# Hymba block on one core: the weight quarters of a Strassen unit are prepared in step with its products

## The chip, the cores and the metric

The kernel runs on one core of one Trainium2 chip. The metric is device time in microseconds (us); the time of a kernel is the median of its runs. A profile is one execution taken by the hardware profiler.

## What is computed

One decoder block over 2048 positions, 1024 features wide, in float32. Cut to what matters here:

```python
h = rmsnorm(x, norm1_g)
proj = h @ w_in                       # 1024 -> 3088 columns: q, k, v, g, a, c_b, c_c, c_h
o = rmsnorm(gla_chunked(q, k, v, log_a)) * silu(g)      # gated linear attention, chunked
o_conv = c_b * causal_depthwise_conv(c_c * c_h)         # the short convolution
x = x + concat(o, o_conv) @ w_out
h2 = rmsnorm(x, norm2_g)
x = x + (silu(h2 @ w_ffn_gate) * (h2 @ w_ffn_up)) @ w_ffn_down   # 1024 -> 2816 -> 1024
out = rmsnorm(x, norm_f_g)
```

## The kernel before

**Halves and units.** The sequence is worked in two halves of 1024 positions. Every large matrix product is cut into units. A unit is a 2 by 2 block product by a Strassen-Winograd scheme with seven products instead of eight (`PRODUCTS`): A11·B11, S1·T1, S2·T2, A12·B21, S3·T3, S4·B22, A22·T4. The A side is weights: four raw quarters A11, A12, A22, A21, and the sums S1 to S4, which VectorE (DVE) makes in place from the raw quarters (four operations, line 435). The B side is activations, the operands (`op`), in the same eight forms.

**Split floats.** Each float32 value is used as a high and a low part. `split` makes them: the high part by ScalarE (ACT, line 193), the low part by DVE as the difference (line 194). `product_step` issues three matmuls for each step of 128 in the contracted dimension: high by high, high by low, low by high (lines 460 to 462). A product is 12 matmuls in the input projection and in the FFN's up-projection (four steps), and 6 or 9 in the down-projection (two or three steps, with quarters 256 or 384 columns wide).

**A unit's life.** `raw_weights` loads the four raw quarters with one DMA (pool `rawp`, two buffers; 1024 KB, or 512 and 768 KB in the down-projection). `weight_quarter` splits a quarter into a tile of pool `wqp`, which has four buffers: the split of one quarter can begin when the product four before it has read its own. `unit_weights` writes the whole sequence of splits and sums of a unit ahead of its products: A11, the sums for S1, S2 and S3, S1, S2, A12, S3, the sum for S4, S4, A22. Then `unit` makes the products into PSUM banks and takes the results out: products 0, 1 and 2 by a copy on ACT (`copied`, line 500), later ones by a sum on DVE (`plus`, line 489). Products 0, 2, 4 and 6 accumulate into one bank, 1 and 5 into another, so product 2 must wait for the copy of product 0, product 4 for that of product 2, and so on. In the down-projection the results are mostly added onto a running sum y by DVE (`onto`).

**The order of the kernel.** Opening (norm, transposes, the first input-projection units 0 to 2), the other input-projection units of half 0 (3 to 11) and of half 1 (0 to 11) with the gated attention and its gates worked in between, the output projection, then for each half the FFN: `ffn_up`, 22 units (11 pairs of gate and up), and `ffn_down`, four groups of contracted steps (`GROUPS` = 0, 2, 5, 8) with four units each. The last unit of all, `last_unit`, uses plain quarters without Strassen. The operands of the down-projection were stored to DRAM by `ffn_up`; those named T3, B22 and T4 come back unsplit and are split after the load by ACT and DVE. `load_h2` loads the operands of half 1's up-projection.

**What sets the order on each engine.** A list scheduler with a model of times goes through the program and orders the instructions of each engine by their place in the program and by when they can run. `tc.issue_after` and the helper `behind` only fix which of two instructions of one engine is issued first; they add no semaphore. Each engine works its queue in order, so an instruction that waits holds everything queued behind it on its engine.

Of the kernel before, what the change touches and what calls it, by code (L numbers as in the profile page):

```python
# [11 lines left out]
F32 = mybir.dt.float32  # L12
# [8 lines left out]
P = 128  # L21
D = 1024
SEQ = 2048
PB = 512
# [29 lines left out]
def tile_hymba_block(ctx, tc, x, xt, win, wa, wgu, wout, wffn, wdown, wdown_first, small, out):  # L54
# [270 lines left out]
    def no_operands():  # L325
        return {b: [] for _, b in PRODUCTS}
# [91 lines left out]
    def unit_weights(src, raw=None, between=()):  # L418
# [33 lines left out]
        halves.clear()  # L452
        return w

    def product_step(o, w, op, k, first):
        n = len(op)
        c = slice(k * P, (k + 1) * P)
        wh, wl = w[:, 0, c], w[:, 1, c]
        xh, xl = op[k][:, 0, :], op[k][:, 1, :]
        pe.matmul(o[:], wh, xh, start=first and k == 0, stop=False, skip_group_check=True)  # L460
        pe.matmul(o[:], wh, xl, start=False, stop=False, skip_group_check=True)  # L461
        return pe.matmul(o[:], wl, xh, start=False, stop=k == n - 1, skip_group_check=True)  # L462

    def unit(src, ops, into=None, onto=None, raw=None, between=(), rest=None):

        w = unit_weights(src, raw, between)
        unit_splits[:] = last_hi + last_lo
        with behind(unit_splits):  # L470
            for y, o in unsplit:
                split(y[:], o[:, 0, :], o[:, 1, :])
        unsplit.clear()

        def mul(i, o=None):
            first = o is None
            o = bank() if first else o
            n, m = PRODUCTS[i]
            for k in range(len(ops[m])):
                product_step(o, w[n], ops[m], k, first)  # L480
            tick()
            return o

        def plus(t, o):
            if ordered:
                queued(dve, lambda: dve.tensor_tensor(t[:], o[:], t[:], ALU.add))
            else:
                with behind(held if rest is not None else []):
                    last_plus[:] = [dve.tensor_tensor(t[:], o[:], t[:], ALU.add)]  # L489
            return t  # L490

        def then():
            if rest is not None:
                next(rest)

        def copied(name, o, at):
            if onto is not None:
                return plus(onto[at], o)
            t = tt(name) if into is None else into[at]
            last_out[:] = [act.activation(t[:], o[:], AF.Copy)]  # L500
            return t


        oa = mul(0)
        c11 = copied("c11", oa, (0, 0))
        ob = mul(1)
        c22 = copied("c22", ob, (1, 1))
        mul(2, oa)
        c12 = copied("c12", oa, (0, 1))
        o = mul(3)  # L510
        then()
        plus(c11, o)
        mul(4, oa)
        then()
        plus(c22, oa)
        if rest is not None:
            next(rest, None)
            w["A22"] = weight_quarter(w["A22"])
            held[:] = last_hi + last_lo
            ordered.clear()  # L520
        mul(5, ob)
        plus(c12, ob)
        mul(6, oa)
        if into is not None or onto is not None:
            copied("c21", oa, (1, 0))
        return [(0, 0, c11, False), (1, 1, c22, False), (0, 1, c12, False), (1, 0, oa, True)]

    def settled(c, in_psum):
# [480 lines left out]
    def in_proj(half, ops, raw=None, between=(), rest=None):  # L1009
        def units():  # L1010
            if half == 0:
                yield unit(win[2], ops, raw=raw, between=between, rest=rest)
            for u in range(0 if half else 3, 12):
                yield unit(win[u], ops)

        units = units()
        for dst, i0 in ((s_kq, 0), (s_kq, 2), (s_v, 0), (s_v, 2)):
            if half == 0 and dst is s_kq:
                continue
            for r, j, c, p in next(units):  # L1020
                store(dst[2 * half + j][i0 + r][:], settled(c, p)[:])
        for i0 in (0, 2):
            for r, j, c, p in next(units):
                store(s_g[2 * half + j][i0 + r][:], silu(c, p)[:])
        if half:
            background.append(gla_half(half))
        for i0 in (0, 2):
            cc = {(r, j): settled(c, p) for r, j, c, p in next(units)}
            ch = {(r, j): c for r, j, c, _ in next(units)}
            for r in range(2):  # L1030
                i = i0 + r
                left = halo[:, i, :]
                for j in range(2):
                    s = tp.tile([P, PB + 2], F32, name="u", tag="t")
                    dve.tensor_tensor(s[:, 2:], ch[r, j][:], cc[r, j][:], ALU.mult)
                    act.activation(s[:, 0:2], left, AF.Copy)
                    left = s[:, PB : PB + 2]
                    y = cc[r, j]
                    act.activation(y[:], s[:, 0:PB], AF.Copy, scale=col(C_CW + i))
                    for n in (1, 2):  # L1040
                        dve.scalar_tensor_tensor(
                            y[:], s[:, n : n + PB], col(C_CW + 4 * n + i), y[:], ALU.mult, ALU.add
                        )
                if half == 0:
                    act.activation(halo[:, i, :], left, AF.Copy)
            for r, j, c, _ in next(units):
                y = cc[r, j]
                dve.tensor_tensor(y[:], c[:], y[:], ALU.mult)
                hi = tp.tile([P, PB], F32R, name="hi", tag="t")
                split(y[:], hi[:], y[:].bitcast(F32R))  # L1050
                dst = s_mix[2 * half + j][i0 + r]
                store(dst[:, 0, :], hi[:].bitcast(F32))
                store(dst[:, 1, :], y[:])
# [239 lines left out]
        yield from combine(lambda k, j: s_x1[2 + j][k][:], C_G2, rb, put)  # L1293

    def load_h2():
        ops, loads = no_operands(), raw_loads[-2]
        for _, n in PRODUCTS:
            for k in range(4):
                with tc.issue_after(loads.ins):
                    o = (load_whole if n in WHOLE else load_pair)(s_h2p[n][k])  # L1300
                ops[n].append(o)
        return ops

    def ffn_up(half, ops):
        for m in range(NF // 2):
            us = unit(wffn[2 * m], ops)
            sg = {(r, j): silu(c, p) for r, j, c, p in us}
            for r, j, c, _ in unit(wffn[2 * m + 1], ops):
                s = sg[r, j]
                dve.tensor_tensor(s[:], c[:], s[:], ALU.mult)  # L1310
            b11, b12, b21, b22 = [sg[r, j] for r in range(2) for j in range(2)]
# [24 lines left out]
    def act_op(half, m, n):  # L1336
        return (load_whole if n in WHOLE else load_pair)(s_act[half][m][n])

    def ffn_down(half):
# [6 lines left out]
        for u, m0 in enumerate(GROUPS):  # L1346
            ms = range(m0, m0 + (3 if u else 2))
            last = m0 == LAST_GROUP
            if last:
                drain_background()  # L1350
            raw = None
            if u:
                raw = raw_weights(wdown[4 * u - 4])
                with tc.issue_after(raw_loads[-1].ins):
                    ops = {n: [group_op(m, n) for m in ms] for _, n in PRODUCTS}
            else:
                ops = {n: [group_op(m, n) for m in ms] for _, n in PRODUCTS}
# [3 lines left out]
                    tiny.tile([P, PB], F32, name=f"ssx{j}", tag=f"ssx{j}", bufs=1) for j in range(2)  # L1361
                ]
            for d0 in range(0, KD, 2):
                src = wdown[4 * u - 4 + d0 // 2] if u else wdown_first[d0 // 2]
                if u == 0 and d0 == 2:

                    order = [(m, n) for _, n in PRODUCTS for m in range(GROUPS[1], GROUPS[2])]
# [2 lines left out]
                if u == 0:  # L1370
                    for d in (d0, d0 + 1):
                        if d < KD - 1:
                            pair = opp.tile([P, 2, PB], F32, name="y", tag="op")
                        for j in range(2):
                            y[d, j] = pair[:, j, :] if d < KD - 1 else bt("y")[:]
                    unit(src, ops, {(r, j): y[d0 + r, j] for r in range(2) for j in range(2)})
                    continue
                xs = []
                if u < 3:
# [1 line left out]
                        xs.append((y[d, u - 1], bt("x1")))  # L1381
                        load(xs[-1][1][:], s_x1[2 * half + u - 1][d][:])
                if last and half and d0 == KD - 2:
                    last_unit(src, ops, [act_op(half, m, "B12") for m in ms], y, ssq)
                    break
                onto = {(r, j): y[d0 + r, j] for r in range(2) for j in range(2)}
                unit(src, ops, onto=onto, raw=None if d0 else raw)
                for r, j in ((0, 0), (1, 1), (0, 1), (1, 0)):
                    yy = onto[r, j]
                    if last and half:  # L1390
# [24 lines left out]
                dve.scalar_tensor_tensor(y[:], y[:], col(C_GF + d), rb[:], ALU.mult, ALU.mult)  # L1415
                store(out[2 * half + j, :, d, :], y[:])

    def last_unit(src, ops, b12, y, ssq):


        raw = raw_weights(src)
        w = [weight_quarter(raw[:, i, :]) for i in (0, 1, 3, 2)]
        columns = (ops["B11"], ops["B21"]), (b12, ops["B22"])
        def gain(d, j):
            return act.activation(y[d, j], y[d, j], AF.Copy, scale=col(C_GF + d))
# [101 lines left out]
        ctx.enter_context(tc.tile_pool(name=n, bufs=bufs, reuse_waits="tile"))  # L1527
        for n, bufs in (("fx", 11), ("fo", 3))
    ]
    for half in range(2):  # L1530
        ffn_up(half, load_h2() if half else h2)
        ffn_down(half)
# [106 lines left out]
```

## Time and profile before

| | before |
|---|---|
| median of 3 runs | 2059.78 us (2059.01 to 2061.59) |
| the profiled execution | 2056.94 us, its span 2055.2 us |
| granted TensorE clock | 0.995 |
| ScalarE table loads at line 540 | 8, of 1283 ns each |
| operations in the splits at line 193 (raw quarters) | 612, 587 ns each |
| their low parts at line 194 | 612, 739 ns each |

In a profile PE is TensorE's matmuls, PEld its weight loads, DVE VectorE, ACT ScalarE, POOL GpSimd and SP the queue that issues the DMAs. A row of the timeline gives the start (us from the start of the span), the duration, the engine, the source line, the operation and its tiles, output left of the arrow; in brackets how long the engine was idle before it and what ended that. Equal neighbours are put together (x2). A row of the waits gives an engine's line, what it waited for, the total, the number of waits and the longest. Lines are those of the kernel before.

### The profile page before, as it was taken

Reading aid. Unit: us, or ns where it says so; the run is one execution under the profiler, and the core shown is the slowest. Engines: PE = TensorE matmul, PEld = TensorE weight load, DVE = VectorE, ACT = ScalarE, POOL = GpSimd, SP = SyncE. Lnnn points to the kernel's source line nnn. Section 1 sums busy time; section 2 is a strip of 40 time slices with the busy share of each in tenths; the row PEclk is TensorE's granted clock in tenths of the full one; section 3 lists DMA queues with packets and bytes.
Section 4 is the critical chain, followed back from the end, with each engine's and each line's share of the span. In section 5 each row is a group of like instructions: output and inputs, shape, how many; then the busy total and the mean of one; then the engine's idle time right before and its main releaser. Section 6 shows DMA issues by size and latency. Waiting matters only on the chain.

```text
span 2055.2 us, 27032 instructions
## 1 busy us (share of the span) xinstructions
PE 2024.1 (98%) x9271; PEld 1664.6 (81%) x9271; DVE 1548.4 (75%) x2533; ACT 979.9 (48%) x1934; POOL 336.4 (16%) x218
## 2 busy tenths in 40 slices
PE   9999999999999999999999999999999999999997
PEld 8778878787888888888888888887888878888886
DVE  7878976569743787887786788877777777778884
ACT  6665455766543344444444552335544544453344
POOL 0000000000002451232131112201312221211213
PEclk9999999999999999999999999999999999999999
DMA  7356786425686873555454676576544534486663
GB/s 261 116 196 214 281 303 194 140 75 170 221 275 218 327 273 123 207 182 205 159 181 147 236 277 253 190 279 249 180 148 169 188 125 169 168 323 215 241 226 117
DMA packets 189738, 422.54 MB, mean 206 GB/s; under 512 B 19904, under 2 KB 65184, under 8 KB 180128
## 3 DMA queue, kind: packets, MB, share of 16 engines
q1 hardware_dynamic: 189600, 420.81, 57.8%
q8 instruction: 73, 1.20, 0.2%
q14 instruction: 65, 0.53, 0.1%
HBM read 276.02 MB, written 144.70 MB: 205 GB/s over the span
## 4 chain that ended last, share of the span: by engine, by line
PE 86%; DVE 5%; DMA 4%; ACT 3%; issue 2%; SPq 0%; POOL 0%; DVEq 0%; ACTq 0%; POOLq 0%
PE mm L460 25%; PE mm L462 24%; PE mm L461 24%; DMA op<-sa_T 2%; PE mm L1201 2%; PE mm L1202 2%; PE mm L1204 2%; DVE wq L194 1%; DMA raw<-in_wffn_dram 1%; DVE h L882 1%; PE a_ps L958 1%; PE mm L744 1%; PE mm L746 1%; PE mm L745 1%; PE o_ps L1125 1%
## 5 line engine op out<-in xcount | busy, mean ns | idle before, releaser
L460 PE MATMUL mm<-op,wq 128*128 128x512 f32 x2467 | 961.7, 393 | 13.7 <-ACT c L500 6.6
L461 PE MATMUL mm<-op,wq 128*128 128x512 f32 x2467 | 960.8, 390 | 0.2 <-DVE op L194 0.2
L462 PE MATMUL mm<-op,wq 128*128 128x512 f32 x2467 | 951.2, 390 | 0.5 <-DVE wq L194 0.2
L193 ACT ACTIVATE wq<-raw 128x512 fp32r<-128x512 f32 (+2 forms) x612 | 355.4, 587 | 588.3 <-PE mm L462 456.5
L194 DVE TENSOR_TENSOR wq<-raw,wq 128x512 fp32r<-128x512 f32 (+2 forms) x612 | 449.1, 739 | 179.7 <-ACT wq L193 177.8
L460 PEld LDWEIGHTS mm<-op,wq 128*128 128x128 f32 x2467 | 464.2, 188 | 118.2 <-ACT c L500 8.5
L462 PEld LDWEIGHTS mm<-op,wq 128*128 128x128 f32 x2467 | 464.2, 188 | 100.1 <-DVE wq L194 2.4
L461 PEld LDWEIGHTS mm<-op,wq 128*128 128x128 f32 x2467 | 464.3, 188 | 96.1 <-DVE op L194 1.3
L1183 POOL TENSOR_TENSOR ssx<-ssx,q 128x512 f32<-128x512 f32 x52 | 74.8, 1453 | 867.6 <-ACT q L1182 867.4
L489 DVE TENSOR_TENSOR c<-mm,c 128x512 f32<-128x512 f32 x196 | 134.8, 688 | 56.2 <-PE mm L462 53.7
L489 DVE TENSOR_TENSOR y<-mm,y 128x512 f32<-128x512 f32 x185 | 126.5, 687 | 47.4 <-PE mm L462 47.1
L435 DVE TENSOR_TENSOR raw<-raw 128x512 f32<-128x512 f32 (+2 forms) x192 | 151.7, 794 | 3.2
L1314 POOL TENSOR_TENSOR t<-c,c 128x512 f32<-128x512 f32 x44 | 73.9, 1678 | 432.0 <-DVE c L1310 409.7
L500 ACT ACTIVATE c<-mm 128x512 f32<-128x512 f32 x198 | 115.5, 588 | 19.0 <-PE mm L462 15.8
L1201 PE MATMUL mm<-op,wq 128*128 128x512 f32 x256 | 100.7, 395 | 0.0
L435 DVE TENSOR_TENSOR s<-raw 128x512 f32<-128x512 f32 (+2 forms) x96 | 64.1, 668 | 48.3 <-DMA raw<-in_wffn_dram 23.7
L1202 PE MATMUL mm<-op,wq 128*128 128x512 f32 x256 | 99.9, 390 | 0.0
L193 ACT ACTIVATE wq<-s 128x512 fp32r<-128x512 f32 (+2 forms) x96 | 56.2, 586 | 88.9 <-PE mm L462 85.3
L1396 POOL TENSOR_TENSOR y<-x,y 128x512 f32<-128x512 f32 x32 | 58.3, 1823 | 229.8 <-DVE y L489 163.7
L1204 PE MATMUL mm<-op,wq 128*128 128x512 f32 x256 | 79.9, 390 | 0.0
L435 DVE TENSOR_TENSOR raw<-s,raw 128x512 f32<-128x512 f32 (+2 forms) x96 | 69.8, 727 | 1.9
L194 DVE TENSOR_TENSOR op<-op 128x512 fp32r<-128x512 f32 x94 | 62.0, 686 | 5.3 <-ACT op L193 5.0
(230 smaller groups left out, 1777.4 us busy)
## 6 DMA issues: line engine op xcount, KB each, us to landing
raw<-in_wffn_dram SPq DMA_DIRECT2D x44, 1024.0 KB, 6.1
sa_B<-so SPq DMA_DIRECT2D x47, 512.0 KB, 3.4
op<-sa_B SPq DMA_DIRECT2D x47, 512.0 KB, 7.1
raw<-in_win_dram SPq DMA_DIRECT2D x22, 1024.0 KB, 5.4
sa_T<-so SPq DMA_DIRECT2D x44, 512.0 KB, 4.2
op<-sa_T SPq DMA_DIRECT2D x44, 512.0 KB, 6.6
raw<-in_wdown_dram SPq DMA_DIRECT2D x24, 768.0 KB, 5.6
sx<-y SPq DMA_DIRECT2D x48, 256.0 KB, 4.2
```

The source lines that it names most:

```text
L193: last_hi[:] = [act.activation(hi, src, AF.Copy)]
L194: last_lo[:] = [dve.tensor_tensor(lo, src, hi.bitcast(F32), ALU.subtract)]
L435: dve.tensor_tensor(*args)
L460: pe.matmul(o[:], wh, xh, start=first and k == 0, stop=False, skip_group_check=True)
L461: pe.matmul(o[:], wh, xl, start=False, stop=False, skip_group_check=True)
L462: return pe.matmul(o[:], wl, xh, start=False, stop=k == n - 1, skip_group_check=True)
L489: last_plus[:] = [dve.tensor_tensor(t[:], o[:], t[:], ALU.add)]
L500: last_out[:] = [act.activation(t[:], o[:], AF.Copy)]
L1183: pool.tensor_tensor(ssq[:], ssq[:], q[:], ALU.add)
L1201: pe.matmul(o[e, j][:], wh, m[:, 0, :], start=k == 0, stop=False)
L1202: pe.matmul(o[e, j][:], wh, m[:, 1, :], start=False, stop=False)
L1204: pe.matmul(o[e, j][:], wl, ops[k][j][:, 0, :], start=False, stop=k == KD - 1)
```

## The change

The weights of all units after the opening's are no longer prepared by the unit itself. A generator, `weight_flow`, goes over a list of weight sources, once for the input projection and once for the whole FFN, both halves, and yields once per quarter. `begin_flow` starts it with four credits; `advance` runs it as far as credits allow; after each product's copy or sum `unit` calls `freed`, which gives one credit (for the narrow quarters of group 0, of which two share a tile, one for every two). So the split of quarter p + 4 is written right behind the copy or sum of product p, and fixed behind it on its engine by `behind(last_out + last_plus)`. The sums stand with the splits: the sum that makes S1 behind the split of A11, the two others ahead of the split of S1, the last with S3. The raw load of the next unit is written when a unit's flow begins, so that the flow is two loads ahead (`Begun`). `load_h2` is put behind an earlier weight load (`raw_loads[-4]`), the operand loads of the down-projection behind the load of the unit that is just beginning, and `last_unit` finds its quarters already made.

```diff
+    plan, begun_units, credits, flowing = deque(), deque(), [0], []
+    class Begun:
+        def __init__(self, src):
+            self.raw = raw_weights(src)
+            self.load = raw_loads[-1]
+            self.w, self.narrow = {}, src.shape[-1] == PB // 2
+    def weight_flow():
+        following = Begun(plan.popleft())
+        while following is not None:
+            u, following = following, None
+            begun_units.append(u)
+            if plan:
+                following = Begun(plan.popleft())
...
+                s1 = rawp.tile([P, PB], F32, name="s1", tag="s1", bufs=1)[:, 0:n]
+                jobs = [
+                    ("A11", a11, [(s1, a21, a22, ALU.add)]),
+                    ("S1", s1, [(a21, a11, a21, ALU.subtract), (a11, s1, a11, ALU.subtract)]),
+                    ("S2", a11, ()), ("A12", a12, ()),
+                    ("S3", a21, [(a12, a12, a11, ALU.subtract)]), ("S4", a12, ()),
+                    ("A22", a22, ()),
+                ]
+            for i, (name, part, sums) in enumerate(jobs):
+                yield not (u.narrow and i % 2)
+                with behind(last_out + last_plus):
+                    if name == "S1":
+                        for job in sums:
+                            dve.tensor_tensor(*job)
+                    w[name] = weight_quarter(part)
+                    if name != "S1":
+                        for job in sums:
+                            dve.tensor_tensor(*job)
...
+    def advance():
+        while flowing:
+            fresh = flowing[1]
+            if fresh and not credits[0]:
+                return
+            credits[0] -= fresh
+            flowing[1:] = [next(flowing[0], None)]
+            if flowing[1] is None:
+                flowing.clear()
+    def begin_flow(sources):
+        plan.extend(sources)
+        credits[0] = 4
+        flow = weight_flow()
+        flowing[:] = [flow, next(flow)]
+        advance()
...
-        w = unit_weights(src, raw, between)
+        flows = src is None
+        if flows:
+            current = begun_units.popleft()
+            w = current.w
+        else:
+            w = unit_weights(src, raw, between)
...
+        def freed(i):
+            if flows and flowing:
+                if not current.narrow or i % 2 or i == len(PRODUCTS) - 1:
+                    credits[0] += 1
+                advance()
...
         oa = mul(0)
         c11 = copied("c11", oa, (0, 0))
+        freed(0)
         ob = mul(1)
         c22 = copied("c22", ob, (1, 1))
+        freed(1)
...
-        ops, loads = no_operands(), raw_loads[-2]
+        ops, loads = no_operands(), raw_loads[-4]
...
-                raw = raw_weights(wdown[4 * u - 4])
-                with tc.issue_after(raw_loads[-1].ins):
+                with tc.issue_after(begun_units[0].load.ins):
                     ops = {n: [group_op(m, n) for m in ms] for _, n in PRODUCTS}
...
-    def last_unit(src, ops, b12, y, ssq):
-        raw = raw_weights(src)
-        w = [weight_quarter(raw[:, i, :]) for i in (0, 1, 3, 2)]
+    def last_unit(ops, b12, y, ssq):
+        w = [begun_units[0].w[i] for i in (0, 1, 3, 2)]
```

More of the change, by code (lines that the diff above doesn't have):

```diff
@@ L453, in unit_weights @@
         return w
+    plan, begun_units, credits, flowing = deque(), deque(), [0], []
[11 more added lines that the diff above has]
+                following = Begun(plan.popleft())
+            raw, w, n = u.raw, u.w, u.raw.shape[-1]
+            a11, a12, a22, a21 = [raw[:, i, :] for i in range(4)]
+            if following is None and last_plain:
+                jobs = [(i, raw[:, i, :], ()) for i in (0, 1, 3, 2)]
+            else:
[17 more added lines that the diff above has]
+                            dve.tensor_tensor(*job)
+            halves.clear()
+    last_plain = []
+    def advance():
[13 more added lines that the diff above has]
+        advance()
     def product_step(o, w, op, k, first):
@@ L464, in unit @@
     def unit(src, ops, into=None, onto=None, raw=None, between=(), rest=None):
-        w = unit_weights(src, raw, between)
+        flows = src is None
+        if flows:
+            current = begun_units.popleft()
+            w = current.w
+        else:
+            w = unit_weights(src, raw, between)
         unit_splits[:] = last_hi + last_lo
@@ L505, in unit @@
         c11 = copied("c11", oa, (0, 0))
+        freed(0)
         ob = mul(1)
         c22 = copied("c22", ob, (1, 1))
+        freed(1)
         mul(2, oa)
         c12 = copied("c12", oa, (0, 1))
+        freed(2)
         o = mul(3)
@@ L512, in unit @@
         plus(c11, o)
+        freed(3)
         mul(4, oa)
@@ L515, in unit @@
         plus(c22, oa)
+        freed(4)
         if rest is not None:
@@ L522, in unit @@
         plus(c12, ob)
+        freed(5)
         mul(6, oa)
@@ L525, in unit @@
             copied("c21", oa, (1, 0))
+        freed(6)
         return [(0, 0, c11, False), (1, 1, c22, False), (0, 1, c12, False), (1, 0, oa, True)]
@@ L1012, in units @@
                 yield unit(win[2], ops, raw=raw, between=between, rest=rest)
+                begin_flow([win[u] for h in range(2) for u in range(0 if h else 3, 12)])
             for u in range(0 if half else 3, 12):
-                yield unit(win[u], ops)
+                yield unit(None, ops)
         units = units()
@@ L1305, in ffn_up @@
         for m in range(NF // 2):
-            us = unit(wffn[2 * m], ops)
+            us = unit(None, ops)
             sg = {(r, j): silu(c, p) for r, j, c, p in us}
-            for r, j, c, _ in unit(wffn[2 * m + 1], ops):
+            for r, j, c, _ in unit(None, ops):
                 s = sg[r, j]
@@ L1350, in ffn_down @@
                 drain_background()
-            raw = None
             if u:
-                raw = raw_weights(wdown[4 * u - 4])
-                with tc.issue_after(raw_loads[-1].ins):
+                with tc.issue_after(begun_units[0].load.ins):
                     ops = {n: [group_op(m, n) for m in ms] for _, n in PRODUCTS}
@@ L1363, in ffn_down @@
             for d0 in range(0, KD, 2):
-                src = wdown[4 * u - 4 + d0 // 2] if u else wdown_first[d0 // 2]
                 if u == 0 and d0 == 2:
@@ L1375, in ffn_down @@
                             y[d, j] = pair[:, j, :] if d < KD - 1 else bt("y")[:]
-                    unit(src, ops, {(r, j): y[d0 + r, j] for r in range(2) for j in range(2)})
+                    unit(None, ops, {(r, j): y[d0 + r, j] for r in range(2) for j in range(2)})
                     continue
@@ L1383, in ffn_down @@
                 if last and half and d0 == KD - 2:
-                    last_unit(src, ops, [act_op(half, m, "B12") for m in ms], y, ssq)
+                    last_unit(ops, [act_op(half, m, "B12") for m in ms], y, ssq)
                     break
                 onto = {(r, j): y[d0 + r, j] for r in range(2) for j in range(2)}
-                unit(src, ops, onto=onto, raw=None if d0 else raw)
+                unit(None, ops, onto=onto)
                 for r, j in ((0, 0), (1, 1), (0, 1), (1, 0)):
@@ L1529, in tile_hymba_block @@
     ]
+    last_plain.append(True)
+    begin_flow(
+        [
+            w
+            for _ in range(2)
+            for w in (
+                *[wffn[u] for u in range(NF)],
+                *[wdown_first[d] for d in range(4)], *[wdown[d] for d in range(12)],
+            )
+        ]
+    )
     for half in range(2):
```

## The prediction

> **What bounds the kernel now.** I read the page's first part, then its chain, then what TensorE (PE) waited for.
>
> ```profile
> span 2055.2 us, 27032 instructions
> PE 2024.1 (98%) x9271; PEld 1664.6 (81%) x9271; DVE 1548.4 (75%) x2533; ACT 979.9 (48%) x1934; POOL 336.4 (16%) x218
> ...
> PE 86%; DVE 5%; DMA 4%; ACT 3%; issue 2%; SPq 0%; POOL 0%; DVEq 0%; ACTq 0%; POOLq 0%
> ```
>
> PE is busy for 98% of the span and carries 86% of the chain. The change leaves every matmul in place, so all that it can win lies in the 2055.2 - 2024.1 = 31.1 us in which PE is idle, plus stretches in which PE runs slowly after a wait. What it can lose has no such ceiling. The windows of time show where PE is idle at all:
>
> ```profile
> 770.00:1280.00 510.00, 510.00 (x2262) 422.37 (x2261) 403.38 (x600) 226.72 (x411) 109.25 (x68) 1.00 0.54 195
> ...
> 277.10:281.10 4.00, 3.92 (x11) 3.12 (x12) 2.40 (x4) 2.25 (x5) 0.00 (x0) 0.62 1.05 395
> ...
> 1423.50:1427.50 4.00, 3.93 (x17) 3.27 (x18) 3.12 (x4) 2.47 (x6) 1.29 (x1) 1.00 0.66 229
> ```
>
> The columns are the stretch, its length, busy time (count) of PE, PEld, DVE, ACT and POOL, the granted PE clock, DMA share and GB/s. In the 510 us of the first up-projection half and most of its down-projection PE never stops: 2262 matmuls, 510 / 2262 = 0.2255 us each. So a 12-matmul product is 2.71 us, a 9-matmul one 2.03, a 6-matmul one 1.35. There the change can win nothing. PE's waits sit elsewhere, few and named:
>
> ```profile
> PE mm L460 <- ACT c L500: 6.6, 5, 2.1
> PE mm L460 <- ACT wq L193: 3.0, 3, 1.9
> ...
> PE mm L460 <- DVE c L489: 1.3, 2, 1.1
> ...
> PE mm L460 <- DVE y L489: 0.7, 2, 0.5
> ```
>
> That is 11.6 us in 12 waits: products that wait for the copy or sum that frees or fills their buffer, or for a split weight quarter. This is the class that the change is able to touch. Each time the engine had the wrong thing ahead of the wanted one in its queue, as the next rows show.
>
> **The change, part by part.** On PE, VectorE (DVE), POOL and SP the changed program has the same instructions, reordered; ScalarE (ACT) has four table loads fewer. So the sum is about order.
>
> *Copy ahead of split.* In the timeline at 1423 a split (wq) is issued ahead of the copy (c) that PE wants:
>
> ```profile
> 1421.29 0.63 ACT L193 ACTIVATE wq<-raw 128x512 fp32r<-128x512 f32 x1 [2.70 <-PE mm L462]
> ...
> 1422.41 0.62 ACT L193 ACTIVATE wq<-raw 128x512 fp32r<-128x512 f32 x1
> 1422.93 0.59 ACT L500 ACTIVATE c<-mm 128x512 f32<-128x512 f32 x1
> ...
> 1423.57 0.19 PEld L460 LDWEIGHTS mm<-op,wq 128*128 128x128 f32 x1 [2.12 <-ACT c L500]
> ```
>
> The split at 1421.29 was itself waiting 2.70 us for PE to free its buffer, and the copy stood behind it and another split. In the changed order each copy stands ahead of the split that its product frees. This wait goes: -2.1 us. What is late next is the sum on DVE after product 3, with a product's 2.71 us of cover.
>
> *Table loads.* At 126 and 401 ACT was at table loads and other work when PE wanted it:
>
> ```profile
> 122.19 1.28 ACT L1005 ACT_TABLE_LOAD   x1
> 123.48 0.21 ACT L1005 ACTIVATE el<-g 128x4 f32<-128x4 f32 x1
> ...
> 125.43 0.61 ACT L193 ACTIVATE wq<-raw 128x512 fp32r<-128x512 f32 x1
> ...
> 126.10 0.50 PE L460 MATMUL mm<-op,wq 128*128 128x512 f32 x1 [1.85 <-ACT wq L193]
> ...
> 398.02 1.28 ACT L540 ACT_TABLE_LOAD   x1
> ...
> 399.81 1.14 ACT L193 ACTIVATE wq<-raw 128x512 fp32r<-128x512 f32 x2
> 400.85 0.59 ACT L500 ACTIVATE c<-mm 128x512 f32<-128x512 f32 x1
> 401.49 0.50 PE L460 MATMUL mm<-op,wq 128*128 128x512 f32 x1 [1.83 <-ACT c L500]
> ```
>
> In the new ACT order two loads disappear from the input projection's first half (four become two) and two from its second (twelve become ten). One load ahead of the split at 125.43 takes 1.3 of the 1.85 us: -1.3, bounds 0 and -1.9. At 401 the two splits (1.04 us from start to start) and, where the load at 398.02 is one of those that go, 1.28 us leave the path: bounds 0 and -1.8; I take -1.2, since which load goes there depends on when the neighbours become ready. The Trainium skill's page "ScalarE: Activation LUTs", in "What ACT_TABLE_LOAD costs", adds about 1.38 us of drain to each load's 1.283; four loads would then free 10.6 us of ACT, not 5.1. Here the next instruction begins 0.01 us after the load (122.19 + 1.28, 123.48), so the row is used.
>
> *Sums on DVE.* At 470 PE waited for a sum that stood behind four scans and a weight sum; at 1383 one that stood behind a weight sum waiting for its DMA:
>
> ```profile
> 466.05 1.37 DVE L1000 TENSOR_TENSOR_SCAN g<-ones,g 128x128 f32<-128x128 f32 x4
> ...
> 468.58 0.69 DVE L435 TENSOR_TENSOR raw<-s,raw 128x512 f32<-128x512 f32 x1
> 469.18 0.69 DVE L489 TENSOR_TENSOR c<-mm,c 128x512 f32<-128x512 f32 x1
> 469.92 0.50 PE L460 MATMUL mm<-op,wq 128*128 128x512 f32 x1 [1.11 <-DVE c L489]
> ...
> 1381.63 0.69 DVE L435 TENSOR_TENSOR s<-raw 128x512 f32<-128x512 f32 x1 [3.84 <-DMA raw<-in_wffn_dram]
> ...
> 1383.71 0.50 PE L460 MATMUL mm<-op,wq 128*128 128x512 f32 x1 [0.53 <-DVE y L489]
> ```
>
> In the new order the product's sum precedes both. -1.1 and -0.5, bounds 0 to those. The other price of this part is steady: two weight sums now stand ahead of the S1 split, 0.69 us each. DVE's work per product is 403.38 us / (2262 / 12) = 2.14 us under a product of 2.71, so 0.57 us is free and a buffer has four products' time before it is wanted: taken at nothing. If that cover were gone, one 0.69 us operation per up-projection unit would be 44 x 0.69 = 30 us; the window with no PE idle at all speaks against it.
>
> *The start of half 1 of the input projection.* It has ACT splitting loaded operands (op) ahead of copies:
>
> ```profile
> 275.50 1.14 ACT L193 ACTIVATE op<-op 128x512 fp32r<-128x512 f32 x2
> 276.54 0.58 ACT L500 ACTIVATE c<-mm 128x512 f32<-128x512 f32 x1
> ...
> 277.18 0.50 PE L460 MATMUL mm<-op,wq 128*128 128x512 f32 x1 [2.11 <-ACT c L500]
> ...
> 280.91 0.63 PE L461 MATMUL mm<-op,wq 128*128 128x512 f32 x1
> 281.34 0.45 PE L462 MATMUL mm<-op,wq 128*128 128x512 f32 x1
> ```
>
> After these 2.11 us matmuls begin 0.43 us apart instead of 0.2255, and the granted clock of the four microseconds is 0.62; some eight of them cost 8 x 0.2 = 1.6 us more. The other waits of this list left the clock at 1.00 (the window at 1423). The Trainium skill's page "TensorE: Matmul & The Clock Gate" ("Why this matters for your kernels") allows gaps up to about 3 us before half rate returns; this trace disagrees at 2.11 us, and by the page a wait costs its own length alone. In the new order eight operand splits stand ahead of that copy, not six: 2 x 0.52 (half of 275.50 to 276.54) = +1.0 us, unless the DMAs land earlier. Bounds -2.1 - 1.6 = -3.7 and +2; I take +0.5.
>
> *Operand loads ahead of weight splits at the down-projection's groups.* This is the new wait. At the step from group 0 to group 1, in both halves, three T3 splits, one copy and a B22 split now stand on ACT ahead of the S2 and A12 splits; before, S2 came first:
>
> ```profile
> 1222.64 0.39 PE L460 MATMUL mm<-op,wq 128*128 128x512 f32 x1
> ...
> 1224.73 1.31 ACT L193 ACTIVATE op<-op 128x512 fp32r<-128x512 f32 x2 [1.37 <-DMA op<-sa_T]
> 1225.95 0.51 ACT L193 ACTIVATE wq<-raw 128x384 fp32r<-128x384 f32 x1
> ...
> 1227.40 0.57 ACT L500 ACTIVATE y<-mm 128x512 f32<-128x512 f32 x1
> ...
> raw<-in_wdown_dram SPq DMA_DIRECT2D x24, 768.0 KB, 5.6
> ```
>
> The last row is a DMA's: one size, and the median time to land. PE began S2 at 1222.64; with the A22 product (6 matmuls) now placed ahead of it, it wants A12 or S2 at 1222.64 + 1.35 = 1224.0. On ACT, from the second T3 split: two T3 splits (1225.95 - 1224.73 = 1.22), copy 0.57, B22 0.61, S2 0.51, A12 0.51: 3.4 us. If T3 lands at 1224.73 as before, PE waits 1224.73 + 3.4 - 1224.0 = 4.1 us. But T3's loads wait for the operands of the T2 product, which stands one product earlier in the new PE order (1.35 us), and the 768 KB weight load is issued behind them instead of ahead (5.6 us to land; 4.0 us of traffic at the 195 GB/s of the long window). So the landing is earlier by 1.35 us at the least and 5.4 at the most; I put it at 2.5 to 4: a wait of 0.1 to 1.6 us. I take 0.8, twice: +1.6. The weight load sent later holds up its own sum on DVE and the S4 and A22 splits queued behind it there; the next unit starts at about 1232, so it has some seven microseconds.
>
> *Sum:* -2.1 - 1.3 - 1.2 - 1.1 - 0.5 + 0.5 + 1.6 = **-4.1 us**. The profiled execution took 2056.94 us (span 2055.2 and 1.7 around it), 2.84 below the median of 2059.78; it would go to 2052.8. With the same difference the median becomes **2055.7**, -0.20%. About 0.2% (4.1 us) is what a measurement of this kernel tells from no change; the sum lies on that line.
>
> **Rivals.** *Clean gain:* the new group waits do not appear, the 277 wait shrinks with its slow clock, and smaller waits of the same class (11.6 - 2.1 - 1.9 - 1.8 - 1.1 - 0.5 = 4.2 us, that at 277 among them) go too. 11.6 + 1.6 = 13.2 is its ceiling; at two thirds, 2051. For it: every listed wait has the order as its cause. Against: half of them stand beside DMAs.
>
> *Slower:* at the first group step T3 lands no earlier than before. Each half then waits 4.1 us, more than the 2.11 that brought the slow clock: 4.1 + 1.6 = 5.7, twice 11.4, and +2 at 277. Against gains of 6.2 that is +7.2: 2067. It decides at the landing of the second T3 operand: later than about 1223 of the old time scale, the wait passes 2.1 us, the clock drops, and 2 x 3.7 eats all gains. For it: the DMA share of 1.05 at 277 shows that operand loads fill the queues; against, the weight load leaves their way. By the clock-gate page's limit, also from the Trainium skill, a wait of 4.1 us would slow the matmuls too, so it makes the same of this rival and only moves the deciding point some 1 us later.
>
> *It does not do what it says, or nothing comes of it:* four buffers ring as before, so a split can start no earlier than its buffer frees, before and after; PE is at 98%, and a wait removed in one place is paid at the next DMA. 2059.8.
>
> **Chances.** Forecast 0.45 (its own spread 2052 to 2059, a little over half of it beyond the 0.2% line), clean gain 0.17, slower 0.25, nothing 0.13. Faster by over 0.2%: 0.45 x 0.6 + 0.17 = 0.44. Slower: 0.25, and 0.05 from unseen waits of the DVE order (up to +30): 0.30. Within: 0.26. The range reaches from the clean gain to the slower case: 2049 to 2067.
>
> **What would show it.** Right: the row of PE waiting for c L500 falls from 6.6 to under 3 us; at 126, 401, 470, 1383 and 1423 no wait over 1 us; the first up-projection window still has PE without a gap; no ACT split queued ahead of a copy. Wrong: PE waiting for wq near 1224 or at the same step of half 1 for over 2 us with a clock below 1.00; PE waiting for DVE's c or y by more than 2 us in all; gaps inside 770 to 1280.

## The result: slower by 0.9%

The changed kernel takes 2078.32 us (median of 4 runs, 2075.51 to 2081.11) against 2059.40 us; the ratio is 1.009, 95% interval 1.0078 to 1.0102. A ratio is taken against runs of the kernel before from the same set of measurements (their medians lie between 2058.34 and 2059.43 us) and is not the quotient of two medians, so the two can differ by a tenth of a per cent. The forecast was 2055.7 in a range of 2049 to 2067: wrong in sign and outside the range.

The page of the changed kernel, its first part and its chain:

```profile
span 2075.6 us, 27006 instructions
PE 2032.2 (98%) x9271; PEld 1665.3 (80%) x9271; DVE 1530.8 (74%) x2533; ACT 969.4 (47%) x1930; POOL 325.9 (16%) x218
...
PE 90%; DVE 4%; DMA 3%; ACT 1%; issue 1%; SPq 0%; DVEq 0%; ACTq 0%
```

Lines are now those of the changed kernel: L523 to L525 are the three matmuls of a step (460 to 462 before), L557 the sum after a product (489), L574 the copy (500), L490 and L494 the weight sums (435).

The matmuls are the same 9271, but PE is busy for 8.1 us more (slow stretches count as busy) and idle for 43.4 us, not 31.1. What PE waited for:

```profile
PE rb_ps L238 <- DVE rep L234: 8.9, 2, 5.6
PE mm L525 <- DVE wq L194: 5.4, 6, 1.1
PE mm L523 <- ACT wq L193: 4.9, 2, 4.5
PE mm L523 <- ACT c L574: 3.7, 4, 1.6
PE mm L523 <- ACT op L193: 2.5, 3, 1.8
...
PE mm L523 <- DVE c L557: 0.9, 1, 0.9
```

Copies (c L574) went from 6.6 to 3.7 us, as the change would have it, though not under the 3 us that was forecast. Of the rows that the prediction had no term for, two grew most, both released by DVE: rb_ps, the transposes that spread a row factor (2.3 us before), and L525, the third matmul of a step, which needs the low part of a weight quarter (0.2 before). The long window in which PE had no gap before now reads 500.08 us busy of 510, and 2202 matmuls, not 2262:

```profile
770.00:1280.00 510.00, 500.08 (x2202) 411.63 (x2201) 377.83 (x578) 218.66 (x399) 102.69 (x66) 0.99 0.52 187
```

Three shorter windows, before and then after, show where:

```profile
780.00:830.00 50.00, 50.00 (x234) 41.71 (x233) 37.96 (x74) 21.33 (x39) 13.50 (x7) 1.00 0.40 148
830.00:1100.00 270.00, 270.00 (x1192) 223.63 (x1192) 215.32 (x283) 121.63 (x213) 64.48 (x41) 1.00 0.52 182
1400.00:1450.00 50.00, 47.76 (x209) 38.75 (x208) 41.36 (x58) 29.03 (x52) 12.26 (x8) 1.00 0.58 217
```

```profile
780.00:830.00 50.00, 43.48 (x195) 35.64 (x194) 31.08 (x65) 16.53 (x30) 8.71 (x6) 0.93 0.33 122
830.00:1100.00 270.00, 266.66 (x1174) 219.82 (x1173) 204.75 (x282) 120.41 (x211) 63.76 (x42) 1.00 0.52 184
1400.00:1450.00 50.00, 45.75 (x189) 35.82 (x188) 32.39 (x51) 22.34 (x40) 3.98 (x3) 0.97 0.67 260
```

In the same time PE starts 39, 18 and 20 matmuls fewer; at 0.2255 us each that is 8.8, 4.1 and 4.5 us, 17.4 of the 20.4 us by which the span grew. (The third window does not hold quite the same work in both.) The first two lie in the stretch where PE had no gap before.

**Near 801.** The timeline of DVE: the small steps of lines 230 and 243 to 248, and the copy of line 234 at their end, are the short chain that makes a row factor, on which PE's transposes wait.

```profile
787.74 0.16 DVE L230 TENSOR_SCALAR rs<-rs 128x4 f32<-128x4 f32 x1
...
793.11 0.68 DVE L490 TENSOR_TENSOR raw<-raw 128x512 f32<-128x512 f32 x1
...
793.78 0.68 DVE L194 TENSOR_TENSOR wq<-s,wq 128x512 fp32r<-128x512 f32 x1
...
794.99 0.68 DVE L490 TENSOR_TENSOR raw<-s,raw 128x512 f32<-128x512 f32 x1
...
796.77 1.27 POOL L1396 TENSOR_TENSOR t<-c,c 128x512 f32<-128x512 f32 x1
...
797.06 3.20 DVE L194 TENSOR_TENSOR wq<-raw,wq 128x512 fp32r<-128x512 f32 x2
798.00 1.71 POOL L1396 TENSOR_TENSOR t<-sg,t 128x512 f32<-128x512 f32 x1
...
801.45 0.41 DVE L234 COPY rep<-py 128x512 f32<-128x512 f32 x1
801.92 1.11 PE L238 MATMUL rb_ps<-ident,rep 128*128 128x128 f32 x4 [5.58 <-DVE rep L234]
```

The same chain before, whose transposes do not wait:

```profile
788.92 0.17 DVE L230 TENSOR_SCALAR rs<-rs 128x4 f32<-128x4 f32 x1
...
793.71 0.42 DVE L234 COPY rep<-py 128x512 f32<-128x512 f32 x1
...
796.47 0.60 PE L238 MATMUL rb_ps<-ident,rep 128*128 128x128 f32 x4
```

From first to last the chain takes 801.86 - 787.74 = 14.1 us; before, it took 5.2 (788.92 to 794.13). Between its small steps stand, among others, the weight sums (L490) and low parts (L194) of the next unit. Two low parts take 3.20 us beside two subtractions on GpSimd (POOL), where two otherwise take 1.3. Behind the 5.58 us the granted clock is 0.55 for four microseconds (0.93 over the window of 50), which costs more than another microsecond.

**S4's low part.** The wait comes three times in the first up-projection half, 77.6 us apart; the first of the three:

```profile
887.14 1.62 POOL L1396 TENSOR_TENSOR t<-sg,t 128x512 f32<-128x512 f32 x1 [2.01 <-issue]
...
887.71 1.60 DVE L194 TENSOR_TENSOR so<-sg,so 128x512 fp32r<-128x512 f32 x1
...
888.73 1.74 POOL L359 TENSOR_TENSOR t<-h 128x512 f32<-128x512 f32 x1
...
889.24 1.78 DVE L194 TENSOR_TENSOR so<-h,so 128x512 fp32r<-128x512 f32 x1
...
892.43 1.28 POOL L359 TENSOR_TENSOR h<-h 128x512 f32<-128x512 f32 x1 [1.96 <-DVE h L963]
892.86 1.40 DVE L194 TENSOR_TENSOR wq<-raw,wq 128x512 fp32r<-128x512 f32 x1
894.31 0.50 PE L525 MATMUL mm<-op,wq 128*128 128x512 f32 x1 [1.11 <-DVE wq L194]
```

S4's high part was done at 889.72. DVE comes to the low part 3 us later, after low parts of operands (so), two of them stretched to 1.60 and 1.78 us beside GpSimd subtractions; then it is stretched itself, to 1.40, and PE waits.

**What DVE does instead.** The page's groups of DVE's sum after a product, before and then after; the third figure is DVE's idle time ahead of it, then its releaser:

```profile
L489 DVE TENSOR_TENSOR c<-mm,c 128x512 f32<-128x512 f32 x196 | 134.8, 688 | 56.2 <-PE mm L462 53.7
```

```profile
L557 DVE TENSOR_TENSOR c<-mm,c 128x512 f32<-128x512 f32 x196 | 134.9, 688 | 115.6 <-PE mm L525 110.5
```

DVE stands idle for PE's product twice as long, and is late afterwards. That suggests the theory that I tested: with `behind`, low parts and weight sums are queued behind the sum of a product that PE has not finished, so DVE idles with work in hand, and does it in a heap when others want it. (By the program, the sum is a fresh one for the quarters that products 3, 4 and 5 free. Outside the down-projection products 0 to 2 end in a copy, and on DVE the quarters that they free, S4 among them, stand only behind an older sum; so S4 could be late by the heap, but not by its own mark.) The rival: the four products of lead are too few, whatever the order.

### The profile page after: what moved, and what is told of

Read it like the earlier page. It is cut to its first block, busy times and chain, and to the rows that moved or that the text cites. A ratio compares the mean times of both kernels' runs of the same rounds, so it can differ in the third digit from the quotient of the medians.

```text
span 2075.6 us, 27006 instructions
## 1 busy us (share of the span) xinstructions
PE 2032.2 (98%) x9271; PEld 1665.3 (80%) x9271; DVE 1530.8 (74%) x2533; ACT 969.4 (47%) x1930; POOL 325.9 (16%) x218
## 4 chain that ended last, share of the span: by engine, by line
PE 90%; DVE 4%; DMA 3%; ACT 1%; issue 1%; SPq 0%; DVEq 0%; ACTq 0%
PE mm L523 25%; PE mm L525 25%; PE mm L524 25%; PE mm L1283 3%; PE mm L1286 3%; PE mm L1284 3%; DVE wq L194 1%; DMA op<-shT 1%; DMA raw<-in_win_dram 1%; PE a_ps L1039 1%; PE mm L825 1%; PE mm L827 1%; PE mm L826 1%; PE o_ps L1207 1%; PE o_ps L1209 1%
## 5 line engine op out<-in xcount | busy, mean ns | idle before, releaser
L523 PE MATMUL mm<-op,wq 128*128 128x512 f32 x2467 | 969.0, 394 | 13.3 <-ACT wq L193 4.9
L525 PE MATMUL mm<-op,wq 128*128 128x512 f32 x2467 | 941.4, 391 | 5.5 <-DVE wq L194 5.4
L194 DVE TENSOR_TENSOR wq<-raw,wq 128x512 fp32r<-128x512 f32 (+2 forms) x612 | 444.2, 744 | 205.6 <-ACT wq L193 202.0
L523 PEld LDWEIGHTS mm<-op,wq 128*128 128x128 f32 x2467 | 464.8, 188 | 120.3 <-ACT wq L193 9.9
L525 PEld LDWEIGHTS mm<-op,wq 128*128 128x128 f32 x2467 | 464.4, 188 | 108.3 <-DVE wq L194 10.5
L193 ACT ACTIVATE wq<-raw 128x512 fp32r<-128x512 f32 (+2 forms) x612 | 345.0, 584 | 353.9 <-DVE raw L490 118.9
L557 DVE TENSOR_TENSOR c<-mm,c 128x512 f32<-128x512 f32 x196 | 134.9, 688 | 115.6 <-PE mm L525 110.5
L574 ACT ACTIVATE c<-mm 128x512 f32<-128x512 f32 x198 | 117.6, 594 | 212.4 <-PE mm L525 208.9
L557 DVE TENSOR_TENSOR y<-mm,y 128x512 f32<-128x512 f32 x185 | 126.8, 687 | 57.5 <-PE mm L525 56.8
L1396 POOL TENSOR_TENSOR t<-c,c 128x512 f32<-128x512 f32 x44 | 67.5, 1534 | 442.9 <-DVE c L1392 414.5
L621 ACT ACTIVATE c<-c 128x512 f32<-128x512 f32 x78 | 49.3, 632 | 65.5 <-DVE c L557 64.4
L194 DVE TENSOR_TENSOR wq<-s,wq 128x512 fp32r<-128x512 f32 (+2 forms) x96 | 69.2, 721 | 1.5 <-ACT wq L193 1.5
L194 DVE TENSOR_TENSOR op<-op 128x512 fp32r<-128x512 f32 x94 | 64.3, 719 | 8.0 <-ACT op L193 8.0
L193 ACT ACTIVATE op<-op 128x512 fp32r<-128x512 f32 x94 | 56.3, 624 | 20.6 <-DMA op<-siT 9.1
```

The source lines that it names most:

```text
L193: last_hi[:] = [act.activation(hi, src, AF.Copy)]
L194: last_lo[:] = [dve.tensor_tensor(lo, src, hi.bitcast(F32), ALU.subtract)]
L1396: pool.tensor_tensor(y[:], p[:], q[:], ALU.subtract)
```

## The experiments

**Which half of the kernel.** The flow in one of the two stages alone; the other prepares its weights as before.

```diff
-                begin_flow([win[u] for h in range(2) for u in range(0 if h else 3, 12)])   # e1
...
-                yield unit(None, ops)
+                yield unit(win[u], ops)
...
-            us = unit(None, ops)                         # e2, and so in all of the FFN
+            us = unit(wffn[2 * m], ops)
```

The second run also puts `load_h2` and the operand loads of the down-projection back behind their old loads.

> The flow for the FFN alone; the input projection prepares its weights as before. Adding up the waits of the two profiles region by region, the changed kernel loses about 18 us in the FFN (7 at the transposes of the first row factor near 801, about 6 in waits for the low part of S4, 3 to 4 near 1418 to 1443, the rest in small ones) and about 1 in all in the input projection. Theory 'the FFN's order': 2072 to 2078 us. Rival 'the input projection's wait near 275 upsets all that follows': under 2064.

> The flow for the input projection alone; the FFN prepares its weights as before. Theory 'the FFN's order': 2058 to 2063 us, with the wait near 275 still 4 to 5 us and the one near 126 gone. Rival 'the input projection does it': over 2068.

The FFN alone: 2081.26 us, ratio 1.0107 (1.0082 to 1.0132), 3 us above what was put down. The input projection alone: 2056.36, ratio 0.9986 (0.9976 to 0.9996). The loss is the FFN's, and all of it. In the input projection gains and losses come out a little ahead, though the wait near 275 is 5.00 us there.

**The fixed order.** The same program text, without the marks:

```diff
-                with behind(last_out + last_plus):
+                with behind([]):                 # e3
+                with behind(last_out):           # e5: the mark on ScalarE
+                with behind(last_plus):          # e6: the mark on VectorE
```

> The changed kernel without the rule that fixes each split and sum behind the last copy or sum; the place where they are written stays. Theory 'the place in the program decides, since the scheduler gives each engine what is written first': within 4 us of the changed kernel's 2078. Rival 'the forced order holds back splits that could run': 2060 to 2066, and the waits for the low part of S4 gone.

> The changed kernel with the splits fixed behind the last copy alone (the mark on ScalarE). Theory 'VectorE's mark does the harm: low parts and weight sums stand behind the sum of the product, so they lose the free time ahead of it on the fullest of the helpers': 2056 to 2062. Rival 'ScalarE's mark does it, since the high part comes too late and the low part follows it': 2072 or more.

> The changed kernel with the splits fixed behind the last sum alone (the mark on VectorE). Theory 'VectorE's mark': 2070 to 2080, with the wait of some 5 us at the transposes near 801 still there. Rival 'ScalarE's mark': 2056 to 2062. If both marks are needed, both runs are near 2059.

Without marks: 2059.01 us, ratio 1.0005 (0.9994 to 1.0017); the whole loss is gone, so the place in the program alone does no harm, and my first theory for that run was wrong. With the copy's mark alone: 1.0005 (0.9991 to 1.0018), also nothing. With the sum's mark alone: 2073.10, 1.0060 (1.0041 to 1.0079), and both waits are back:

```profile
PE rb_ps L238 <- DVE rep L234: 8.9, 2, 5.6
PE mm L525 <- DVE wq L194: 6.1, 7, 1.1
```

So the mark on DVE's sum makes most of the loss (0.6 of 0.9%). In the FFN it makes nearly all: between 770 and 2000 us PE starts 5394 matmuls before, 5294 in the changed kernel, 5301 with the sum's mark, 5376 with the copy's and 5386 without marks (one profile each); the run with the sum's mark was further ahead at 770 us. DVE's wait for PE ahead of the sum c follows the mark; without marks, with the copy's, with the sum's:

```profile
DVE c L557 <- PE mm L525: 50.7, 62, 3.5
...
DVE c L557 <- PE mm L525: 52.9, 70, 3.5
...
DVE c L557 <- PE mm L525: 111.0, 105, 4.0
```

**Sums or low parts.** The marks on one kind of DVE's work alone:

```diff
+                if name == "S1":                      # e9: the sums outside behind()
+                    for job in sums:
+                        dve.tensor_tensor(*job)
                 with behind(last_out + last_plus):
-                    if name == "S1":
...
-                    w[name] = weight_quarter(part)    # e10: the split outside behind()
+                w[name] = weight_quarter(part)
+                with behind(last_out + last_plus):
```

> The changed kernel with the four weight sums of a unit no longer fixed behind the product's copy or sum; the splits still are. Theory 'the low parts held behind the sum of the product do the harm': 2070 to 2080, the wait near 801 stays. Rival 'the weight sums held back do it, since the S1 split, and through it the row factor's short chain, wait for them': 2057 to 2063.

> The reverse: the splits free, the weight sums fixed behind the product's copy or sum. Theory 'low parts': 2057 to 2063. Rival 'weight sums': 2068 or more. If both runs fall below 2066, either one alone leaves enough room on VectorE.

With the sums free: 2075.09, 1.0074 (1.0058 to 1.0091). With the splits free: 2060.98, 1.0009 (1.0000 to 1.0019). The windows, sums free and then splits free:

```profile
780.00:830.00 50.00, 49.05 (x229) 40.49 (x228) 37.38 (x73) 21.27 (x38) 12.93 (x7) 1.00 0.39 144
830.00:1100.00 270.00, 266.66 (x1174) 219.89 (x1173) 206.48 (x279) 118.16 (x208) 62.96 (x41) 1.00 0.51 180
```

```profile
780.00:830.00 50.00, 48.98 (x228) 40.59 (x227) 37.55 (x72) 20.84 (x37) 10.88 (x7) 1.00 0.42 158
830.00:1100.00 270.00, 270.00 (x1190) 222.79 (x1190) 207.30 (x285) 120.84 (x214) 63.92 (x41) 1.00 0.50 181
```

Either one clears most of the wait near 801 (229 and 228 matmuls, against 195): the chain needs room on DVE, no matter whose. I had expected it to stay with the sums free. The waits for S4 stay with the sums free and go with the splits free. In time it is the splits that count; of the 34 matmuls that the run with free sums gained near 801 it lost 12 before 770 us and some 19 elsewhere in the FFN.

**GpSimd's part.** GpSimd's four subtractions for each pair of up-projection units become fills, so those operands are zeros:

```diff
-                pool.tensor_tensor(y[:], p[:], q[:], ALU.subtract)
+                pool.memset(y[:], 0.0)
```

> The changed kernel with GpSimd's four subtractions for each pair of up-projection units (T1 to T4 of the activations) replaced by fills of the same tiles, which read nothing; those operands are zeros then. The scheduler's order of VectorE shifts a little. In the changed kernel VectorE's differences of two operands in SBUF take up to 1.78 us beside a subtraction on GpSimd and 0.69 otherwise. Theory 'this slowing makes the low part of S4 late': the waits for S4 (some 5 us) go and the time falls to 2068 to 2074, the 7 us at 801 shrinks. Rival 'order alone': within 3 us of 2078.

2068.10 us, 1.0041 (1.0024 to 1.0058): half of the loss is left. The low parts of gate-times-up (so), in the changed kernel and with fills, by form:

```profile
L194 DVE TENSOR_TENSOR so<-sg,so 128x512 fp32r<-128x512 f32 x22 | 32.6, 1480 | 1.9
```

```profile
L194 DVE TENSOR_TENSOR so<-sg,so 128x512 fp32r<-128x512 f32 x22 | 15.2, 691 | 0.6
```

```profile
780.00:830.00 50.00, 45.39 (x200) 37.02 (x198) 29.91 (x65) 17.34 (x32) 5.21 (x7) 0.93 0.35 132
830.00:1100.00 270.00, 269.83 (x1190) 222.84 (x1189) 190.75 (x285) 121.28 (x213) 37.92 (x50) 1.00 0.52 188
```

1480 ns against 691 for the same instruction, and S4's waits are gone (1190 matmuls against 1174). The wait near 801 is only shorter (3.7 us, not 5.6). The scheduler's order moved a little in this run, so the half is not all GpSimd's. The Trainium skill's page "GPSIMD Engine Reference" ("Specifications") says that its SBUF interfaces are shared with VectorE, with contention for DVE instructions that have two SBUF inputs; the trace agrees: sums that read PSUM (c<-mm) stay at 688 ns in both kernels.

**Lead.** The credits at the start, with the four buffers as they are:

```diff
-        credits[0] = 4
+        credits[0] = 7       # e4; e7: the same, and behind([]); e11: 5; e12: 9
```

> The changed kernel with seven credits at the start, so that each split is written seven products ahead and not four (the four buffers are the same). Theory 'lead': S3, S4 and A22 are now written later than before, behind background work, and their splits lose their place to it; seven ahead, no PE wait for the low part of S4 is left, and the time falls by 6 us or more, to 2063 to 2072. Rival 'the buffers alone decide': no change, 2078.

> Seven ahead and no fixed order together. If lead is what counts and the fixed order only harms where there is little of it, this equals the run with seven ahead, 2050 to 2055. If the two effects add, 2045. If the copies ahead of the splits are what seven ahead gains, it is back at 2056 to 2060.

> Five credits in place of four, the fixed order kept. Theory 'each split wants one product more than the buffers give': most of the loss goes, 2052 to 2062. Rival 'a whole unit's lead is needed': 2068 or more.

> Nine credits. If lead beyond one unit brings nothing, as the four buffers hold the splits back, 2050 to 2055 like seven. If the order still improves with each product of lead, below 2050. If splits written too early push sums and copies aside, 2056 or more.

| credits | order fixed | median, us | ratio (95% interval) |
|---|---|---|---|
| 4 | yes (the change) | 2078.32 | 1.0090 (1.0078 to 1.0102) |
| 5 | yes | 2064.82 | 1.0022 (1.0007 to 1.0037) |
| 7 | yes | 2052.21 | 0.9968 (0.9956 to 0.9980) |
| 9 | yes | 2048.95 | 0.9943 (0.9926 to 0.9959) |
| 4 | no | 2059.01 | 1.0005 (0.9994 to 1.0017) |
| 7 | no | 2053.74 | 0.9970 (0.9953 to 0.9987) |

One product more takes three quarters of the loss, a little less than I had put down for it; seven and nine beat the kernel before, seven by far more than I had put down. Whether nine is better than seven is not clear, as the intervals overlap. With seven, fixing the order makes no difference, which fits a mark on a sum three products further back, long done. So neither theory alone is right: the fixed order costs where the mark is the latest sum, lead removes that cost, and lead also gains by itself. That gain lies in the input projection: by 770 us PE has started 3713 matmuls with seven and 3710 with nine, against 3675 before (38 and 35 more, or 8.6 and 7.9 us), and in the FFN they only keep up (5383 and 5394 between 770 and 2000 us, against 5394). Five ahead it is 3673: waits of 4.33 us at 276 and 3.96 at 301 eat the gain there. The first window and the waits of nine ahead:

```profile
780.00:830.00 50.00, 50.00 (x231) 41.56 (x230) 43.08 (x82) 21.10 (x37) 16.17 (x9) 1.00 0.56 200
```

```profile
ACT c L574 <- PE mm L525: 6.6, 7, 2.8
PE mm L525 <- DVE wq L194: 1.3, 2, 1.2
```

PE has no gap there, and ACT's wait for a product ahead of a copy is 6.6 us, against 208.9 in the changed kernel and 15.8 before: with lead, a split is there to be done when its buffer comes free, not only after the copy. Whether more than nine brings more was not tried.

DVE's idle time ahead of the sum c is a sign of the trouble and not its price: with GpSimd's fills it was 120.0 us at half the loss, and five ahead 42.7 us, less than the 53.7 before, at 1.0022.

## Why the prediction was wrong

**The step that failed** is the one under "Sums on DVE" that took the steady price "at nothing". It set DVE's work per product (2.14 us) against the product's time (2.71) and found room, and it found "a buffer has four products' time before it is wanted". The first is a mean. The second is one product too long: between the product that frees a buffer and the one that wants it stand three. The new rule lets low parts start only after the product's sum, so DVE's free time ahead of the sum no longer counts: its idle time there went from 53.7 to 110.5 us. The step also priced the wrong operations. It asked what the weight sums cost; with the sums free a ratio of 1.0074 was left of 1.0090, with the splits free 1.0009. The low parts held back had no term at all. The bound beside it (+30 us, one weight sum per unit) held the result by luck, since it was reckoned for those sums; and I gave it 5%, because PE had no gap before. That is what the old order had earned, not what the new one would keep. The text named the mark by which this error would show, "gaps inside 770 to 1280".

**GpSimd had no term.** The 0.69 us used for a weight sum is its time when GpSimd is still. Rows of the kernel before already held both figures (low parts of 676 to 1780 ns between 780 and 1280), so the cover was thinner than its mean of 0.57 us where subtractions ran.

**Row factor.** The chain near 801 was not in the sum, nor what would come to stand between its steps on DVE. With its slow clock it is the largest single loss: 5.58 us of waiting and the slow matmuls behind it, some 7 us.

**Copy ahead of split:** right for the rule, not for the place. The term was too large as well: 2.12 us is the idle time in the row of the weight load (PEld), while the matmul's own row has PE waiting 1.69 us. And the wait did not go; one of much the same size stands at 1418, with an operand split as its releaser:

```profile
1418.49 0.49 PE L523 MATMUL mm<-op,wq 128*128 128x512 f32 x1 [1.81 <-ACT op L193]
```

**Table loads:** right. The wait at 126, of 1.85 us, went (-1.3 foreseen), that at 401 fell from 1.83 to 0.64 (-1.2 foreseen). **The sum at 470:** wrong; a wait of 1.61 us for a copy took its place. That at 1383 went.

**Start of half 1:** +0.5 foreseen with a bound of +2; measured 4.46 us of waiting and a granted clock of 0.59, some 2 us more than before:

```profile
275.78 0.50 PE L523 MATMUL mm<-op,wq 128*128 128x512 f32 x1 [4.46 <-ACT wq L193]
```

It waits for a split (wq), which now stands behind operand splits and a copy: the mechanism was right, the size at its bound.

**Groups of the down-projection:** +1.6 foreseen, and no wait of more than 0.3 us at the first step of either half. The loads landed early enough; the "slower" rival had the sign and, with 2067, some two fifths of the size, but from a mechanism that did not occur.

## What to carry to other kernels

An order rule that puts a helper's work behind an event on the critical engine can turn the helper's free time into waiting, even if it adds no semaphore; look at the idle time that the helper has ahead of that event, not at its mean load. What it costs has to be measured, since the idle time alone did not tell it here. If work is to be written in step with a ring of buffers, try writing it well ahead of the ring (seven or nine products for four buffers here) and let the buffers hold it back. And where an engine has no gap at all, ask what in the present order keeps it so before taking that as proof of slack.

## What the hardware showed that I had not expected

A DVE instruction with two SBUF inputs takes 0.69 us with GpSimd still and up to 1.78 beside one of its subtractions, which themselves take 1.3 to 1.8. In the rows near S4's wait each stretched instruction ends 0.55 us behind the end of the subtraction beside it (889.31 and 888.76, 891.02 and 890.47, 894.26 and 893.71), as if it had to wait for that end. The mean over 22 equal ones was 1095 ns in the kernel before, 1480 in the changed one, where they fall otherwise, and 691 with fills on GpSimd. The granted clock over four microseconds from about the end of a wait of PE, in the changed kernel:

```profile
275.70:279.70 4.00, 3.92 (x10) 2.81 (x11) 3.79 (x6) 3.33 (x8) 0.00 (x0) 0.59 0.99 340
...
472.20:476.20 4.00, 3.93 (x17) 3.23 (x18) 4.00 (x9) 3.42 (x10) 0.00 (x0) 1.00 0.41 128
...
1418.40:1422.40 4.00, 3.68 (x9) 2.35 (x10) 3.93 (x7) 3.35 (x8) 0.00 (x0) 0.69 1.07 396
```

and, in the kernel before, from the end of the wait of 1.85 us at 126:

```profile
126.00:130.00 4.00, 3.90 (x19) 3.10 (x20) 3.86 (x10) 3.53 (x6) 0.00 (x0) 1.00 0.16 60
```

A wait of 4.46 us was followed by 0.59 and one of 1.61 us by 1.00; but that at 1418, of 1.81 us and 0.23 more three quarters of a microsecond later, by 0.69, though the longer single waits of 1.85 us at 126 and 1.83 at 401 of the kernel before left 1.00, and its wait of 2.11 us at 277 was followed by 0.62. So a limit on the length of one wait does not tell when the clock drops; what else does was not tried.
